# Hybrid decoder trunk on one Trainium2 core: when projections, table loads and the last gate columns are issued

## Chip, cores and metric

The kernel runs on one core of a Trainium2 chip. The metric is device time in microseconds (us), the median of several executions; less is better. On the engines: PE is TensorE, DVE is VectorE, ACT is ScalarE, POOL is GpSimd, SP is SyncE.

## What is computed

Two identical layers over 512 tokens of width 1024, in float32. `rms_norm` divides by the root mean square; `swiglu` is the feed-forward part. Cut to what matters:

```python
for l in range(DEPTH):                      # DEPTH = 2
    u = rms_norm(x, ln1[l]) @ w_in[l]       # all mixers' inputs and four gates, one product
    y_a = forgetting_attention(...)         # "fox": per-head norms of q and k, 128-query blocks
    y_b = rms_norm(gla_chunked(...)) * silu(gr)
    y_c = rms_norm(retention_chunked(...)) * silu(rg)
    y_d = rms_norm(ssd_chunked(silu(conv(xbc)), ...) * silu(z))
    g = sigmoid(gates)                      # four branches x 1024 columns
    merged = sum(g[b] * (y_b @ w_up_b))     # over the branches a, b, c, d
    x = x + merged @ w_out[l]
    x = x + swiglu(rms_norm(x, ln2[l]), w_ffn_in[l], w_ffn_out[l])
```

## The kernel before

Activations lie transposed in SBUF: 128 partitions of features by 512 tokens, eight such blocks for a row of width 1024. Float32 products are built from float32r pieces: `split` casts a tile to a high part on ACT (L217) and takes the rest as a low part on DVE (L218), and a product of two split operands is three matmuls (`mm`, L203: high by high, low by high, high by low). A projection (`proj`) of 128 columns is eight blocks of three, so 24 matmuls of 128x512 into one PSUM bank named `mm` (four of these banks); the mixers use four other banks named `mx`.

Weights come in slabs of 128x1024 by SP's DMA into `wr` (two buffers). A slab is split into `wh` and `wl` (three buffers each), so ACT's cast of a slab waits until PE has done with the slab three earlier. The feed-forward part and part of `w_in` go through Strassen products, whose low parts are formed by an ACT scaling (L522) and an accumulating DMA from POOL (L523).

ACT holds one set of function tables at a time. `act` puts a table load (L236) ahead of a function from another set and ties the order of the functions with tables: Ln and Exp share a set, Silu and Sin share one, Sigmoid has its own.

One layer runs in this order: the norm of x and its column sums; four projections of C_X side by side (`group`) and two more, each evacuated by DVE with a multiply (L716); a Strassen part; then the four mixers ssd, gla, ret and fox. A mixer is a Python generator: `drain` runs it, and at each yield `pull` takes entries from the list `fill`, each with a cost in us, until the budget PACE of that mixer is used. The entries are independent work for PE: projections of the gate columns (`gate_quad`, four projections each, evacuated at L1370, then a Sigmoid on ACT over a pair tile `k`, 128x1024), projections with a Silu (`silus`), and up-projections (`ups`, evacuated at L1386). What is left over is issued behind fox by `pull(1e9)`.

This sets only the order in which the program is written. The framework's scheduler (`schedule_with_timeline_sim=True`, in `kernel`) then puts the instructions of each engine into a fixed sequence by its own model of time; on the chip each engine works its sequence off in order. SBUF tiles come from pools with fixed counts; `TT()` takes a 128x512 tile from the pool `tp`.

In fox, `fox_squares` squares the four q and k tiles and splits them (L217, L218); a pair of matmuls for each sums the squares over a head (`mx<-t,cr`), Ln and Exp on ACT and three steps on DVE (`newton`, L372 to L374) make the inverse root, and L1247 applies it. `stack` prepares a head (L1255 to L1265), `score` makes a block of scores (DVE L1277 and L1280, Exp on ACT, DVE L1283 and L1284), `value` transposes it (L1293), splits it and multiplies it with v (`mx<-t,t`), and `finish` adds two halves (ACT L1308, DVE L1309) and splits the result `ya`, from which the up-projections of branch a start.

Of the kernel before, what the change touches and what calls it, by code (L numbers as in the profile page):

```python
# [13 lines left out]
AF = mybir.ActivationFunctionType  # L14
# [4 lines left out]
P = 128  # L19
S = 512  # L20
D = 1024
KD = D // P
# [11 lines left out]
C_Z, C_X, C_DT, C_G = 2836, 3348, 4116, 4124  # L34
# [3 lines left out]
WARM = 11  # L38
TILE = 5.2
LAG = 1  # L40
PACE = (4.5, 5.0, 5.0, 7.5)
WIDE = 256 + 28
PARTS = (6, 6, 6, 4)
PLAIN = 2
# [88 lines left out]
def trunk(ctx: ExitStack, tc: tile.TileContext, keys, qkeys, xin, pos, wst, wsq, par, ext, cst, out):  # L133
    nc = tc.nc
# [14 lines left out]
    def nm(s):  # L149
        uid[0] += 1  # L150
        return f"{s}{uid[0]}"

    def pad(pool, n):
        pool.tile([P, n // 4], F32, tag=nm("pad"), name=nm("pad"))
# [8 lines left out]
    def phase(**bufs):  # L163
        st = ExitStack()
        for n, b in bufs.items():
            pools[n] = st.enter_context(tc.tile_pool(name=nm(n), bufs=1 if n[0] == "g" else b, reuse_waits="tile"))
            if n[0] == "g":
                pad(pools[n], b)
            st.callback(pools.pop, n)
        return st  # L170
# [10 lines left out]
    def KT(shape, dtype=F32):  # L181
        return pools["kp"].tile(shape, dtype, tag="k", name=nm("k"))
# [7 lines left out]
    def MM():  # L190
        return pm.tile([P, S], F32, tag="mm", name=nm("mm"))

    def MX():
        return px.tile([P, S], F32, tag="mx", name=nm("mx"))
# [10 lines left out]
    def mm3(o, l, r, start, stop):  # L205
        (lh, ll), (rh, rl) = l, r
        mm(o, lh, rh, start, False)
        mm(o, lh, rl, False, False)
        mm(o, ll, rh, False, stop)
# [19 lines left out]
    def order(a, b):  # L229
        tc.add_manual_dep(a.ins, b.ins.name, mybir.DependencyInfo(mybir.DependencyClass.NoSync, mybir.DependencyReason.DATA), reason="table")  # L230

    def act(out, in_, func, **kw):
        want = {AF.Ln: "natural_log_exp_and_others", AF.Exp: "natural_log_exp_and_others", AF.Silu: "silu_and_others", AF.Sin: "silu_and_others", AF.Sigmoid: "sigmoid_and_others"}.get(func)
        pre = None
        if want and want != seen["set"]:
            pre = A.preload_act_table_set(want)  # L236
            if seen["last"] is not None:
                order(pre, seen["last"])
            seen["set"] = want
            seen["pre"] = pre  # L240
        i = A.activation(out=out, in_=in_, func=func, **kw)  # L241
        if want:
            order(i, seen["pre"])
            seen["last"] = i
        return i
# [184 lines left out]
    def group(name, l, cols, src, nk, hook=None):  # L430
        ps = [MX() for _ in cols]
        for k in range(nk):
            if hook and k in hook:
                hook[k]()
            for i, c in enumerate(cols):
                mm3(ps[i], block(name, l, k, c), src[k], k == 0, k == nk - 1)
        return ps

    def proj(name, l, c, src, nk):
        ps = MM()  # L440
        for k in range(nk):
            mm3(ps, block(name, l, k, c), src[k], k == 0, k == nk - 1)
        return ps
# [173 lines left out]
    def layer(l, n1, scopes):  # L617
        outer, scope = scopes
# [6 lines left out]
        fill = []  # L625
# [10 lines left out]
        def drain(gen, us):  # L636
            for want in gen:
                pull(us * (1 if want is None else want))

        def mix(a, b):  # L640
            n = max(len(a), len(b))
            return [t for i in range(n) for l_ in (a, b) for t in l_[i:i + 1]]
# [32 lines left out]
        gates = {}  # L675
# [32 lines left out]
            begin(-2)  # L708

        ps4 = group("w_in", l, [C_X + P * i for i in range(4)], n1, KD, {4: first, 5: lambda: next(steps), 6: third, 7: fourth})  # L710
        n1.rstd(True)
        for i in range(0, 6, 2):
            t = KT([P, 2, S])
            for j in range(2):
                ps = ps4[i + j] if i < 4 else proj("w_in", l, C_X + P * (i + j), n1, KD)
                V.tensor_tensor(out=t[:, j], in0=ps, in1=n1.r, op=ALU.mult)  # L716
                cin[i + j] = t[:, j]
        cap[0] = len(keys) // SLAB + FRONT // SLAB - 6
        run()
        scope.close()  # L720
        scope = phase(vp=2, bd=1, tp=24)
        vp = pools["vp"]
        sbd = pools["bd"].tile([P, 7, 2, P], F32, name=nm("sbd"))
        G.memset(sbd, 0.0)
# [82 lines left out]
        ps = MX()  # L807
# [538 lines left out]
        def silus(name, c, tiles):  # L1346
            def go(i):
                def f():
                    if i == 0:
                        gates[name] = tiles()  # L1350
                    t = gates[name][i]
                    V.tensor_tensor(out=t, in0=proj("w_in", l, c + P * i, n1, KD), in1=n1.r, op=ALU.mult)
                    act(out=t, in_=t, func=AF.Silu)
                return f
            return [(TILE, go(i)) for i in range(2)]

# [4 lines left out]
        def gate_quad(b, q):  # L1361
            st = {}

            def go(i):
                def f():
                    if i % 2 == 0:
                        st["t"] = KT([P, 2, S])
                        gates.setdefault(b, []).append(st["t"])
                    ps = proj("w_in", l, C_G + b * D + (4 * q + i) * P, n1, KD)
                    V.tensor_tensor(out=st["t"][:, i % 2], in0=ps, in1=n1.r, op=ALU.mult)  # L1370
                    if i % 2:
                        act(out=st["t"], in_=st["t"], func=AF.Sigmoid)
                return f
            return [(TILE, go(i)) for i in range(4)]

# [19 lines left out]
        def up_of(b, q):  # L1395
            ys_, name = {0: (ya, "w_up_a"), 1: (yb, "w_up_b"), 2: (yc, "w_up_c"), 3: (yd, "w_up_d")}[b]
            return ups(b, ys_, name, q, b == 3, b == 0)
# [3 lines left out]
        if l == 0:  # L1401
            rotary()
        drain(ssd(), PACE[0])
        fill += gate_quad(3, 1) + mix(silus("rg", C_RG, lambda: [TT(), TT()]), up_of(3, 0))
        fill += [keep(fq, j, C_FQ + P * j) for j in range(2)] + [keep(fk, j, C_FK + P * j) for j in range(2)]
        drain(gla(), PACE[1])
        fill += [(0.0, fox_sums)] + tokmajor(fv, C_FV, True) + [(0.0, fox_rows)]
        fill += mix(gate_quad(1, 0), up_of(3, 1)) + mix(gate_quad(1, 1), up_of(1, 0))
        drain(ret(), PACE[2])
        fill += mix(gate_quad(2, 0), up_of(1, 1)) + mix(gate_quad(2, 1), up_of(2, 0)) + mix(gate_quad(0, 0), up_of(2, 1)) + gate_quad(0, 1)  # L1410
        drain(fox(), PACE[3])
        fill += up_of(0, 0) + up_of(0, 1)
        pull(1e9)

        n2 = Norm(PR("ln2"), 16)
# [16 lines left out]
        scope = phase(g=128, tq=1, ep=8, rp=5, g0=64, lp=2, g1=384, fp=9)  # L1432
# [25 lines left out]
        ps4 = group("w_ffn_in", l, [0, FFN, P, FFN + P], n2, KD, {4: hook})  # L1458
# [10 lines left out]
        for part, n in enumerate(PARTS):  # L1469
# [17 lines left out]
            ps4 = [MX() for _ in range(4)]  # L1487
# [8 lines left out]
            for d in range(4, KD):  # L1496
                ps = MM()
# [10 lines left out]
    n1 = Norm(pr[:, 0, o:o + w])  # L1508
# [4 lines left out]
    for l in range(DEPTH):  # L1513
        n1 = layer(l, n1, scopes if l == 0 else front())
# [71 lines left out]
```

## Time and profile before

| what | value |
|---|---|
| median of 3 runs | 1767.44 us (1767.35 to 1768.34) |
| the profiled execution | 1772.7 us, span of its records 1770.8 us |
| mean granted clock of TensorE | 0.985 |
| PE busy | 1726.9 us, 98% |
| DVE, ACT, POOL busy | 1250.3, 972.5, 244.5 us |
| table loads (L236) | 80, of 1283 ns each |

The profiled execution is 5.3 us above the median, and 1.9 us of it lie outside the span. A row of the timeline gives start and duration, engine, line, operation, output and inputs, and in brackets the idle time before it and what ended that. Matmuls overlap: a duration of 0.39 us with starts 0.23 us apart means one matmul every 0.23 us. The windows' table gives, for each stretch, its length, the busy time of PE, PE's weight loads, DVE, ACT and POOL with their counts in parentheses, and then the granted TensorE clock (1.00 is full speed), the share of the DMA engines and GB/s.

### The profile page before, as it was taken

How to read it: one execution, taken by the hardware profiler on the slowest of the kernel's cores; microseconds unless marked ns; L12 is line 12 of the kernel's file. 1: busy time of each engine (PE TensorE's matmuls, PEld its weight loads, DVE VectorE, ACT ScalarE, POOL GpSimd, SP SyncE). 2: the span in 40 equal slices, each digit the busy share in tenths (PEclk: the TensorE clock that was granted, in tenths of full speed). 3: DMA queues.
4: the chain of work that ended last, by engine and by line, in shares of the span. 5: the costliest groups of instructions: out<-in, count | busy, mean ns of one | idle time of the engine just before them, and what ended most of it. 6: DMA issues, size and time to landing. Idle time of an engine off the chain costs nothing.

```text
span 1770.8 us, 25962 instructions
## 1 busy us (share of the span) xinstructions
PE 1726.9 (98%) x10428; PEld 1503.6 (85%) x10428; DVE 1250.3 (71%) x1739; ACT 972.5 (55%) x1329; POOL 244.5 (14%) x239
## 2 busy tenths in 40 slices
PE   8999999989989999999999999998998999999998
PEld 6988888768878989898979878886787789999998
DVE  6795776687658767675787766656776687676766
ACT  7656552466637646464665456325656376464643
POOL 2103112022101000000011042010221010101010
PEclk9999999999989999999999999999999899999999
DMA  7432222212215757575344322222122147575743
GB/s 247 96 117 75 72 72 84 81 63 84 84 61 154 191 131 183 133 184 120 96 143 108 107 61 84 82 76 82 60 87 81 60 145 201 128 185 131 188 109 106
DMA packets 56424, 201.34 MB, mean 114 GB/s; under 512 B 6256, under 2 KB 6640, under 8 KB 56304
## 3 DMA queue, kind: packets, MB, share of 16 engines
q1 hardware_dynamic: 45072, 160.45, 28.4%
q0 software_dynamic: 10368, 37.75, 12.1%
q8 instruction: 82, 1.34, 0.3%
q10 hardware_dynamic: 864, 1.48, 0.2%
q14 instruction: 38, 0.31, 0.1%
HBM read 197.56 MB, written 2.10 MB: 113 GB/s over the span
## 4 chain that ended last, share of the span: by engine, by line
PE 85%; DVE 6%; ACT 5%; issue 3%; DMA 1%; POOL 0%; ACTq 0%; POOLq 0%
PE mm L203 55%; PE mx L203 29%; DVE wl L218 1%; ACT L236 1%; ACT wh L217 1%; ACT t L241 1%; ACT k L241 1%; ACT t L217 0%; DVE xl L399 0%; DMA wl<-in_wsq_dram 0%; DVE x L1481 0%; PE mx L1293 0%; DVE f L1480 0%; DVE rq L513 0%; ACT xh L241 0%
## 5 line engine op out<-in xcount | busy, mean ns | idle before, releaser
L217 ACT CAST wh<-wr 128x1024 fp32r<-128x1024 f32 (+1 forms) x228 | 237.2, 1041 | 309.4 <-PE mm L203 159.6
L203 PE MATMUL mm<-xh,wh 128*128 128x512 f32 (+1 forms) x1088 | 389.7, 358 | 1.7 <-DVE k L1370 1.4
L203 PE MATMUL mm<-xh,wl 128*128 128x512 f32 (+1 forms) x1088 | 389.2, 358 | 1.1 <-DVE wl L218 1.1
L203 PE MATMUL mm<-xl,wh 128*128 128x512 f32 (+1 forms) x1088 | 388.3, 357 | 0.0
L218 DVE TENSOR_TENSOR wl<-wr,wh 128x1024 fp32r<-128x1024 f32 (+1 forms) x204 | 254.6, 1249 | 100.5 <-ACT wh L217 98.9
L203 PEld LDWEIGHTS mm<-xh,wh 128*128 128x128 f32 x1088 | 206.4, 190 | 32.2 <-DVE k L1370 1.3
L203 PEld LDWEIGHTS mm<-xh,wl 128*128 128x128 f32 x1088 | 205.8, 189 | 32.4 <-DVE wl L218 2.0
L203 PEld LDWEIGHTS mm<-xl,wh 128*128 128x128 f32 x1088 | 206.3, 190 | 29.3 <-issue 0.5
L203 PE MATMUL mx<-xh,wh 128*128 128x256 f32 (+1 forms) x512 | 154.3, 310 | 6.0 <-ACT wh L217 5.0
L203 PE MATMUL mx<-xl,wh 128*128 128x256 f32 (+1 forms) x512 | 157.5, 308 | 0.0
L203 PE MATMUL mm<-t,wh 128*128 128x512 f32 x448 | 146.8, 405 | 9.2 <-ACT t L217 4.1
L523 POOL DMA_DIRECT2D wl<-in_wsq_dram x70 | 60.4, 864 | 597.9 <-ACT wl L522 403.7
L218 DVE TENSOR_TENSOR l<-rq,wh 128x1024 fp32r<-128x1024 f32 x72 | 87.9, 1221 | 40.7 <-ACT wh L217 24.8
L203 PEld LDWEIGHTS mm<-t,wh 128*128 128x128 f32 x448 | 85.1, 193 | 29.2 <-ACT t L217 4.5
L203 PE MATMUL mx<-f,wh 128*128 128x512 f32 x352 | 108.2, 390 | 0.0
L203 PEld LDWEIGHTS mx<-xh,wh 128*128 128x128 f32 x512 | 97.2, 190 | 12.6 <-ACT wh L217 6.1
L203 PE MATMUL mm<-f,wh 128*128 128x512 f32 x352 | 105.9, 389 | 0.0
L217 ACT CAST wh<-rq 128x1024 fp32r<-128x1024 f32 x72 | 75.5, 1048 | 51.2 <-PE mm L203 22.4
L236 ACT ACT_TABLE_LOAD x80 | 102.6, 1283 | 1.3
L203 PEld LDWEIGHTS mx<-xl,wh 128*128 128x128 f32 x512 | 97.3, 190 | 5.4
L203 PE MATMUL mx<-xh,wl 128*128 128x256 f32 (+1 forms) x304 | 95.4, 325 | 0.8 <-DVE wl L218 0.4
L203 PE MATMUL mm<-t,wl 128*128 128x512 f32 x224 | 89.7, 400 | 0.0
(308 smaller groups left out, 3816.2 us busy)
## 6 DMA issues: line engine op xcount, KB each, us to landing
wr<-in_wst_dram SPq DMA_DIRECT2D x200, 512.0 KB, 3.5
rq<-in_wsq_dram SPq DMA_DIRECT2D x72, 512.0 KB, 5.6
wl<-in_wsq_dram POOLq DMA_DIRECT2D x70, 512.0 KB, 6.5
wr<-in_wsq_dram SPq DMA_DIRECT2D x24, 512.0 KB, 7.0
out_dram<-x SPq DMA_DIRECT2D x8, 256.0 KB, 2.0
x<-in_x_dram SPq DMA_DIRECT2D x3, 512.0 KB, 6.4
wr<-in_wst_dram SPq DMA_DIRECT2D x4, 256.0 KB, 5.4
l<-in_wsq_dram POOLq DMA_DIRECT2D x2, 512.0 KB, 6.9
```

Of the source, the lines that this page charges most:

```text
L203: T.matmul(o, lhsT=l, rhs=r, start=start, stop=stop, skip_group_check=True)
L217: A.copy(out=hi, in_=src)
L218: V.tensor_tensor(out=lo, in0=src, in1=hi.bitcast(F32), op=ALU.subtract)
L236: pre = A.preload_act_table_set(want)
L241: i = A.activation(out=out, in_=in_, func=func, **kw)
L523: G.dma_start(out=lo, in_=wsq[j], accum_op=ALU.add)
```

## The change

Seven edits. PACE goes from 4.5, 5, 5, 7.5 to 4.4, 4.9, 4.9, 7.2. The fifth projection of C_X is written ahead of `n1.rstd(True)`, so its matmuls may stand between the group and the norm's column sums. The mixers' pool `tp` gets 28 tiles instead of 24 (8 KB more of each partition). Both Silus of a `silus` pair are issued with the second projection, and both Sigmoids of a `gate_quad` with its fourth. The last two projections of the last `gate_quad(0, 1)` are taken out of the list that fox pulls from and written behind fox, ahead of branch a's up-projections. The memory set aside for the descriptors of dynamic transfers is 8192 instead of 16384 bytes, so tiles lie 8 KB lower.

```diff
-PACE = (4.5, 5.0, 5.0, 7.5)
+PACE = (4.4, 4.9, 4.9, 7.2)
...
         ps4 = group("w_in", l, [C_X + P * i for i in range(4)], n1, KD, {4: first, 5: lambda: next(steps), 6: third, 7: fourth})
+        ps4.append(proj("w_in", l, C_X + 4 * P, n1, KD))
         n1.rstd(True)
...
-                ps = ps4[i + j] if i < 4 else proj("w_in", l, C_X + P * (i + j), n1, KD)
+                ps = ps4[i + j] if i + j < 5 else proj("w_in", l, C_X + P * (i + j), n1, KD)
...
-        scope = phase(vp=2, bd=1, tp=24)
+        scope = phase(vp=2, bd=1, tp=28)
...
                     V.tensor_tensor(out=t, in0=proj("w_in", l, c + P * i, n1, KD), in1=n1.r, op=ALU.mult)
-                    act(out=t, in_=t, func=AF.Silu)
+                    if i:
+                        for t in gates[name]:
+                            act(out=t, in_=t, func=AF.Silu)
...
-                    if i % 2:
-                        act(out=st["t"], in_=st["t"], func=AF.Sigmoid)
+                    if i == 3:
+                        for t in gates[b][-2:]:
+                            act(out=t, in_=t, func=AF.Sigmoid)
...
-        fill += mix(gate_quad(2, 0), up_of(1, 1)) + mix(gate_quad(2, 1), up_of(2, 0)) + mix(gate_quad(0, 0), up_of(2, 1)) + gate_quad(0, 1)
+        last_quad = gate_quad(0, 1)
+        fill += mix(gate_quad(2, 0), up_of(1, 1)) + mix(gate_quad(2, 1), up_of(2, 0)) + mix(gate_quad(0, 0), up_of(2, 1)) + last_quad[:2]
         drain(fox(), PACE[3])
-        fill += up_of(0, 0) + up_of(0, 1)
+        fill += last_quad[2:] + up_of(0, 0) + up_of(0, 1)
...
-    nc = _bacc.Bacc("TRN2", target_bir_lowering=False, num_devices=1)
+    nc = _bacc.Bacc("TRN2", target_bir_lowering=False, num_devices=1, dynamic_dma_scratch_size=8192)
```

The scheduler orders all engines anew. In ACT's sequence the rows at L236 go from 80 to 48. Lines of the changed file are up to 5 higher: L1370 becomes L1373, L1386 becomes L1390, L1247 becomes L1248, L1308 becomes L1309.

**Place 1, the start of fox in layer 0.** ACT before, from the cast of a slab to the last of the four squares (t_3173, t_3179, t_3185 and t_3191 in this listing are the squares; wh608 and wh617 are slabs, t540 and t543 belong to the norm of ret's heads):

```order
L217 CAST wh608_3408<-wr607_3406 128x1024
L217 CAST t540_3111<-t537_3099 128x512
L217 CAST wh617_3456<-wr616_3454 128x1024
L217 CAST t543_3122<-t538_3102 128x512
L241 ACTIVATE t551_3173<-t425_2486 128x512
L217 CAST t552_3175<-t551_3173 128x512
L241 ACTIVATE t554_3179<-t432_2525 128x512
L217 CAST t555_3181<-t554_3179 128x512
L241 ACTIVATE t557_3185<-t453_2601 128x512
L217 CAST t558_3187<-t557_3185 128x512
L241 ACTIVATE t560_3191<-t462_2646 128x512
```

ACT after; the slab cast of the same place is wh617, the squares are t545, t548, t551, t554:

```order
L217 CAST t543_3116<-t538_3096 128x512
L241 ACTIVATE t545_3120<-t427_2486 128x512
L217 CAST t546_3122<-t545_3120 128x512
L241 ACTIVATE t548_3126<-t448_2562 128x512
L217 CAST t549_3128<-t548_3126 128x512
L241 ACTIVATE t551_3132<-t457_2607 128x512
L217 CAST t552_3134<-t551_3132 128x512
L241 ACTIVATE t554_3138<-t466_2656 128x512
L217 CAST wh617_3448<-wr616_3446 128x1024
L217 CAST t555_3140<-t554_3138 128x512
```

The cast of slab wh617 stood ahead of all squares and of the last split of ret's norm; it now stands behind three squares, ahead of the fourth's cast. In PE's sequence the last matmuls of that norm (`mx<-t,cr`) were followed by 4 matmuls of one gate projection, 6 of an up-projection and 24 of the next projection; now by 5, 24, 6 and 24. Behind them come 6 of an up-projection and the fox norms as before, but these 6 now stand between the second norm's two matmuls, and the stack's matmul stands ahead of the next gate projection (g2qa below) instead of inside it.

DVE before, from the last split of a square on; mm563 is the bank of an up-projection which g2qa takes over:

```order
L218 TENSOR_TENSOR t562_3194<-t560_3191,t561_3193 128x512
L1386 TENSOR_TENSOR t567_3210<-mm563_3197,k493_2831 128x512
L372 SCALAR_TENSOR_TENSOR t581_3271<-mx573_3249,t577_3261 128x512
L372 SCALAR_TENSOR_TENSOR t582_3277<-mx574_3252,t578_3264 128x512
L373 SCALAR_TENSOR_TENSOR t581_3271<-t581_3271,t577_3261 128x512
L373 SCALAR_TENSOR_TENSOR t582_3277<-t582_3277,t578_3264 128x512
```

DVE after; the same bank is mm576 here, read in the row at L1390 with t580:

```order
L218 TENSOR_TENSOR t556_3141<-t554_3138,t555_3140 128x512
L372 SCALAR_TENSOR_TENSOR t572_3214<-mx564_3193,t568_3205 128x512
L372 SCALAR_TENSOR_TENSOR t573_3220<-mx565_3196,t569_3207 128x512
L373 SCALAR_TENSOR_TENSOR t572_3214<-t572_3214,t568_3205 128x512
L373 SCALAR_TENSOR_TENSOR t573_3220<-t573_3220,t569_3207 128x512
L372 SCALAR_TENSOR_TENSOR t574_3226<-mx566_3199,t570_3209 128x512
L374 SCALAR_TENSOR_TENSOR t568_3205<-t572_3214,t568_3205 128x512
L372 SCALAR_TENSOR_TENSOR t575_3232<-mx567_3202,t571_3211 128x512
L1390 TENSOR_TENSOR t580_3250<-mm576_3237,k497_2839 128x512
L1390 TENSOR_TENSOR t586_3292<-mm585_3285,k497_2839 128x512
L1390 TENSOR_TENSOR t593_3335<-mm592_3328,k521_2998 128x512
```

The evacuation that frees the bank stood ahead of the Newton steps of the fox norms; it now stands behind seven of them, the first step of the fourth norm (t575) among them, and two more evacuations follow it at once.

**Place 2, the end of fox in layer 0.** ACT before, from the Exp of the last block of scores (t823) on; k817 is a gate pair tile, t831 and t834 are the split of the transposed scores, t836 to t837 the finish:

```order
L241 ACTIVATE t823_4446,frs825_4453<-t823_4446,fmx824_4451 128x512
L236 ACT_TABLE_LOAD
L241 ACTIVATE k817_4410<-k817_4410 128x1024
L236 ACT_TABLE_LOAD
L217 CAST t831_4496<-mx830_4491 128x512
L217 CAST t834_4508<-mx833_4504 128x384
L1308 COPY t836_4516<-mx813_4397 64x512
L217 CAST t837_4519<-t719_3951 128x512
```

ACT after; the last Exp is t814, the gate pairs are k808 and k830, the split is t822 and t825, the finish t827 and t828:

```order
L241 ACTIVATE t814_4364,frs816_4371<-t814_4364,fmx815_4369 128x512
L236 ACT_TABLE_LOAD
L241 ACTIVATE k808_4328<-k808_4328 128x1024
L217 CAST wh860_4572<-wr859_4570 128x1024
L241 ACTIVATE k830_4439<-k830_4439 128x1024
L236 ACT_TABLE_LOAD
L217 CAST t822_4412<-mx821_4407 128x512
L217 CAST t825_4424<-mx824_4420 128x384
L1309 COPY t827_4432<-mx802_4305 64x512
L217 CAST t828_4435<-t713_3894 128x512
```

Between the last Exp and the split stood a table load, a Sigmoid and a table load; now a slab cast (wh860) and a second Sigmoid stand there too. PE, between the last score and the products of the split (`mx<-t,t`, eight matmuls), had 8 matmuls of the last gate projection and 12 of the up-projections of branch a; now it has all 24 of the last projection and 12 of the up-projections. In layer 1 the last score stood behind the whole projection and 9 matmuls of the up-projections, with 3 left between it and the products; after, both layers have the order of layer 0. The wait of wh860 is for the last projection's last matmul, and that of Sigmoid k830 for that projection's evacuation on DVE.

**Place 3, the norm of layer 1.** PE before, from the last matmuls of the group on; mm1511 is the bank of the norm's sum, mm1522 that of the fifth projection:

```order
L203 MATMUL mx1484_8507<-xl1428_8279,wh1495_8581 128x512
L203 MATMUL mx1484_8507<-xh1427_8278,wl1496_8582 128x512
L203 MATMUL mm1511_8674<-n1512_8675,cr_123 128x512
L203 MATMUL mm1514_8681<-cs_122,n1437_8343 128x1 x4
L203 MATMUL mm1522_8708<-xh1427_8278,wh1507_8638 128x512
L203 MATMUL mm1522_8708<-xl1428_8279,wh1507_8638 128x512
L203 MATMUL mm1522_8708<-xh1427_8278,wl1508_8639 128x512
L203 MATMUL mm1522_8708<-xh1427_8278,wh1507_8638 128x512
```

PE after; the fifth projection is mm1511, the sum mm1515:

```order
L203 MATMUL mx1484_8491<-xl1428_8263,wh1495_8565 128x512
L203 MATMUL mx1484_8491<-xh1427_8262,wl1496_8566 128x512
L203 MATMUL mm1511_8658<-xh1427_8262,wh1507_8622 128x512
L203 MATMUL mm1511_8658<-xl1428_8263,wh1507_8622 128x512
L203 MATMUL mm1515_8689<-n1516_8690,cr_123 128x512
L203 MATMUL mm1518_8696<-cs_122,n1437_8327 128x1 x4
L203 MATMUL mm1511_8658<-xh1427_8262,wl1508_8623 128x512
L203 MATMUL mm1511_8658<-xh1427_8262,wh1507_8622 128x512
```

Two of the fifth projection's matmuls now precede the sum; the third, which reads the slab's low part, follows it.

## Prediction

> **What bounds it now.** I read the page first: the share of each engine, the chain that ended last, the table loads.
>
> ```profile
> span 1770.8 us, 25962 instructions
> PE 1726.9 (98%) x10428; PEld 1503.6 (85%) x10428; DVE 1250.3 (71%) x1739; ACT 972.5 (55%) x1329; POOL 244.5 (14%) x239
> PE 85%; DVE 6%; ACT 5%; issue 3%; DMA 1%; POOL 0%; ACTq 0%; POOLq 0%
> L236 ACT ACT_TABLE_LOAD x80 | 102.6, 1283 | 1.3
> ```
>
> PE is busy for 98%, and the chain lies on it for 85%. The change takes no matmul away, so it can win only what PE waits (1770.8 - 1726.9 = 43.9 us) and what PE loses at a lower clock. Next I asked the windows where that is: the start of fox and its end, in layer 0 and in layer 1.
>
> ```profile
> 345.00:400.00 55.00, 48.06 (x194) 36.81 (x193) 45.16 (x66) 35.06 (x48) 11.73 (x9) 0.94 0.21 67
> 478.00:510.00 32.00, 27.46 (x114) 22.10 (x113) 18.71 (x30) 13.17 (x19) 0.58 (x2) 0.84 0.21 65
> 1220.00:1275.00 55.00, 48.81 (x194) 37.05 (x193) 43.31 (x65) 35.29 (x49) 9.21 (x8) 0.94 0.20 62
> 1355.00:1390.00 35.00, 28.15 (x116) 22.20 (x115) 18.35 (x31) 16.88 (x24) 1.45 (x2) 0.80 0.19 60
> ```
>
> In these 177 us PE idles for 6.94 + 4.54 + 6.19 + 6.85 = 24.5 us, over half of all. The clock column gives the rest: (1 - 0.94) x 55 = 3.3, (1 - 0.84) x 32 = 5.1, again 3.3, and (1 - 0.80) x 35 = 7.0 us of full clock not granted. The timeline of PE at the start of fox, layer 0, shows each wait and both speeds:
>
> ```profile
> 351.40 0.39 PE L203 MATMUL mm<-xl,wh 128*128 128x512 f32 x1
> 351.63 0.39 PE L203 MATMUL mm<-xh,wl 128*128 128x512 f32 x1
> 353.49 0.73 PE L203 MATMUL mm<-t,wh 128*128 128x512 f32 x2 [1.47 <-DVE k L1370]
> ...
> 358.21 0.50 PE L203 MATMUL mx<-t,cr 128*128 128x512 f32 x1 [3.07 <-ACT t L217]
> ...
> 364.11 0.63 PE L203 MATMUL mm<-xh,wl 128*128 128x512 f32 x1
> 364.54 0.63 PE L203 MATMUL mm<-xh,wh 128*128 128x512 f32 x1
> ```
>
> A matmul follows another after 0.23 us at full clock (351.40, 351.63) and after 0.43 at the lower one (364.11, 364.54). The 1.47 us wait was not followed by the lower clock, the 3.07 us one was.
>
> **Part 1: the end of fox (the term that decides).** Timelines of PE, ACT and DVE in layer 0, and of PE in layer 1:
>
> ```profile
> 489.36 0.77 PE L1293 MATMUL mx<-cs,t 128*128 128x128 f32 x5
> 492.48 2.48 PE L203 MATMUL mx<-t,t 128*128 128x256 f32 x8 [2.35 <-ACT t L217]
> 497.00 2.50 PE L203 MATMUL mm<-t,wh 128*128 128x512 f32 x5 [2.04 <-ACT t L217]
> ```
> ```profile
> 486.40 1.05 ACT L217 CAST wh<-wr 128x1024 fp32r<-128x1024 f32 x1 [4.33 <-issue]
> 487.35 0.72 ACT L241 ACTIVATE t<-t,fmx 128x512 f32<-128x512 f32 x1
> ...
> 488.18 1.28 ACT L236 ACT_TABLE_LOAD   x1
> 489.48 1.06 ACT L241 ACTIVATE k<-k 128x1024 f32<-128x1024 f32 x1
> 490.55 1.28 ACT L236 ACT_TABLE_LOAD   x1
> 491.85 0.97 ACT L217 CAST t<-mx 128x512 fp32r<-128x512 f32 x2
> 495.00 0.58 ACT L1308 COPY t<-mx 64x512 f32<-64x512 f32 x1 [2.19 <-PE mx L203]
> 496.33 0.62 ACT L217 CAST t<-t 128x512 fp32r<-128x512 f32 x1 [0.75 <-DVE t L1309]
> ```
> ```profile
> 484.39 0.75 DVE L1277 SCALAR_TENSOR_TENSOR t<-mx,cq,t 128x512 f32<-128x512 f32 x1 [1.41 <-PE mx L203]
> ```
> ```profile
> 1369.58 1.33 PE L1293 MATMUL mx<-cs,t 128*128 128x128 f32 x5 [2.25 <-DVE t L1284]
> 1373.12 2.48 PE L203 MATMUL mx<-t,t 128*128 128x256 f32 x8 [2.22 <-ACT t L217]
> 1377.70 2.50 PE L203 MATMUL mm<-t,wh 128*128 128x512 f32 x5 [2.09 <-ACT t L217]
> ```
>
> The split at 491.85 has its input from 490.13 (489.36 + 0.77), yet stands behind a Sigmoid between two table loads. What it costs now: layer 0 waits 2.35 + 2.04, and of the 10.2 us at half clock (twice 5.1) some 2.0 are idle, so 8.2 us do 4.1 us' worth; 2.35 + 2.04 + 4.1 = 8.5. Layer 1 waits 2.25 + 2.22 + 2.09, and 14.0 us at half clock less 4.3 idle cost 4.8: 11.4.
>
> After, by the new order with these durations, counted from the score's end S (484.2, before DVE's 484.39): the Exp starts at S + 3.15 and ends at S + 3.9 (487.35 + 0.72); a slab cast and the table load run by then as before. The cast wh860 must wait for the last of 24 projection matmuls, S + 6.3 (24 x 0.23 and three small ones, and 0.4 to drain). The first Sigmoid is done by S + 6.3 too (3.9 + 0.2 + 1.28 + 1.06). Then the cast 1.05, Sigmoid 1.06, load 1.28: S + 9.7; the products follow 0.65 later (491.83 to 492.48), S + 10.3. PE is ready for them after 36 matmuls of 0.23 and about 1.0 of small ones, S + 9.3. So one wait of about 1.0 us stays of the first, in both layers. The finish (product, copy L1308, L1309, cast) is not touched: 2.04 stays, nothing is put behind it. Whether 1.0 and 2.0 with 0.9 us of products between them lower the clock, no row shows; it costs from nothing to the present 4.1 and 4.8, and I take 2.0, in the middle. New cost per layer 1.0 + 2.04 + 2.0 = 5.0. Gain 8.5 - 5.0 + 11.4 - 5.0 = **9.9 us**, ends 5.0 (clock as now) and 13.9 (full clock). The two projections put behind fox thus help by standing inside this wait: 36 instead of 20 matmuls of cover, for 2.1 us more of ACT work.
>
> Here 2.35 and 2.04 in succession did lower the clock (0.84 in the window), while 1.47 alone did not. The Trainium skill ("TensorE: Matmul & The Clock Gate", HAM oscillation) asks for no idle gap over about 3.4 us; by it neither wait would lower the clock, and the gain would be the 13.9 end. On waits of this length this trace does not agree with it.
>
> **Part 2: the start of fox.** ACT and DVE in layer 0:
>
> ```profile
> 354.95 1.04 ACT L217 CAST wh<-wr 128x1024 fp32r<-128x1024 f32 x1 [4.06 <-PE mm L203]
> 356.36 0.62 ACT L217 CAST t<-t 128x512 fp32r<-128x512 f32 x1 [0.36 <-DVE t L851]
> ...
> 361.62 1.84 ACT L241 ACTIVATE t<-mx,cs 128x512 f32<-128x512 f32 x3
> 363.33 1.15 ACT L241 ACTIVATE t<-t 128x512 f32<-128x512 f32 x2
> ```
> ```profile
> 356.19 1.22 DVE L218 TENSOR_TENSOR wl<-wr,wh 128x1024 fp32r<-128x1024 f32 x1
> ...
> 362.35 0.68 DVE L1386 TENSOR_TENSOR t<-mm,k 128x512 f32<-128x512 f32 x1
> 364.00 1.29 DVE L372 SCALAR_TENSOR_TENSOR t<-mx,t 128x512 f32<-128x512 f32 x2 [0.97 <-ACT t L241]
> ```
>
> Now the squares are late because the slab cast (354.95) waited 4.06 us for PE and everything on ACT queued behind it: PE waits 1.47 + 3.07 and loses 3.3 by the clock; of the window's other 2.4 us of idle time I let 1.0 go, since two more evacuations now follow the first at once on DVE: 8.8 per layer. After, three squares stand ahead of that cast, and PE has 24 more matmuls (5.5 us) before the fox norms: both waits go. What is late next: the fourth square's split, behind cast wh617 (1.04 + 0.62 on ACT, a slab's low part 1.22 and the split 0.7 on DVE, from about 0.2 after the up-projection's last matmul), against 0.9 us of PE work: about 2.4 us. Then the next gate projection needs a bank that DVE frees only behind the fourth norm's first Newton step: Ln 0.61, two Exp 1.15, L372 0.65, L1390 0.68 and 0.3 of hand-overs, less one matmul, 3.2 us. 5.6 us of waits and some 3.3 of clock: 8.9. **Nothing is won, 0 us**; ends -4 and +6 for both layers.
>
> **Part 3: the fifth projection.** PE at the norm of layer 1:
>
> ```profile
> 910.22 0.50 PE L203 MATMUL mm<-n,cr 128*128 128x512 f32 x1 [2.73 <-ACT n L217]
> ...
> 912.73 0.80 PE L203 MATMUL mm<-xh,wl 128*128 128x512 f32 x1 [0.58 <-DVE wl L218]
> ```
>
> Two of its matmuls now run in the 2.73 us, but the third still waits for the slab's low part until 912.73. The two waits end where they did: 0, at most -0.5 (two matmuls).
>
> **Part 4: the rest.** 32 of 80 table loads go, 41 us of ACT at 1.283; ACT has 45% idle, so most of it is hidden, and parts 1 and 2 have what I could place. PE's other waits are 43.9 - 24.5 = 19.4 us, the program's start and part 3 included. Fewer loads may win some, but a pair of Sigmoids now holds ACT for 4.7 us (2 x 1.28 + 2 x 1.06) instead of 3.6: **-2 us**, ends -6 and +5. "ScalarE: Activation LUTs" of the Trainium skill (What ACT_TABLE_LOAD costs) adds a drain of 1.38 us to each load's 1.28, which would double ACT's saving; here the Sigmoid starts 0.02 us behind its load (488.18 + 1.28, 489.48), so no drain is added. The smaller PACE and the four tiles: 0, since the list is empty before the fox ends either way, and no wait of the rows above is for a `tp` tile.
>
> ```profile
> L523 POOL DMA_DIRECT2D wl<-in_wsq_dram x70 | 60.4, 864 | 597.9 <-ACT wl L522 403.7
> wl<-in_wsq_dram POOLq DMA_DIRECT2D x70, 512.0 KB, 6.5
> ```
>
> Half the descriptor memory touches only these 70 accumulating transfers. POOL idles 597.9 us before them, mostly for ACT, so a later issue has room; were one held until the last landed (6.5 us), a few would reach PE. 0, up to +3; a gain has no row to come from.
>
> **Sum.** -9.9 + 0 + 0 - 2 = -12 us, 1772.7 to 1760.7 of the profiled execution, which is 5.3 above the median: 1767.44 to **1755**.
>
> **Rivals.** *All waits at both places go, with the clock:* 8.5 + 11.4 + 2 x 8.8 = 37.5, 1730. For it: half of ACT's excursions are gone. Against: the finish's 2.04 us is untouched. *The clock stays up at fox's end:* 1.0 and 2.0 are too short for it; the gain there is 13.9 and the whole -16, 1751. For it: 1.47 us did nothing. Against: 2.35 and 2.04 sufficed. This is what the skill's rule above gives.
>
> *It does not do what it says:* the scheduler puts the last projections almost where they were, and every wait moves on by one; 0, 1767. For it: parts 2 and 3. Against: 36 matmuls against 20, and in layer 1 against 3. *Slower, by the bank at fox's start:* if the evacuation waits for all seven Newton steps ahead of it and not only for the last, 6 x 0.65 = 3.9 us are added per layer, and a half-clock stretch 1.7 more, 11 for both; with the 5 of part 1's low end that gives +6, 1773. It decides as soon as ACT's Ln rows start more than 3 us later than PE is done with the third norm. For it: DVE works in order, and nothing else is ready behind. Against: the first three norms' sums come before the slab cast.
>
> **Chances.** My case 0.51, the clock stays up 0.15, all waits gone 0.05, no change 0.12, slower 0.17. What a measurement of this kernel can tell from no change is 0.2%, 3.5 us. With every term at its better end the sum is -13.9 - 4 - 0.5 - 6 = -24.4, 1743; that is the low end, and leaves out the first rival. At their worse ends the terms give -5 + 6 + 5 + 3 = +9, beyond the slower rival's +6; I cut at +3.6, 1771, which holds no change and leaves out most of the slower cases, some 0.12. My case alone I put at -4 to -20. Faster 0.71, same 0.12, slower 0.17.
>
> **What would show it.** Part 1: 36 matmuls after the last score, then a wait near 1 us, one near 2.0, and a clock above 0.84 and 0.80 in these windows. Part 2: no wait at the first fox norm, 2 to 3 us at the fourth, 3 us before the next gate projection behind DVE's L1390. Part 3: the third matmul waits for `wl`. I am wrong if the two end windows gain under 5 us, or if the start windows lose more than 6.

## The result, and the profile after

The changed kernel takes 1756.49 us (median of 4 runs, 1755.23 to 1758.37), the kernel before 1767.8 beside it (4 runs, 1767.35 to 1768.34): ratio 0.9928, interval 0.9916 to 0.9941. The ratio is the recorded one; the two medians by themselves give 0.9936, inside the interval. 1755 was predicted. From its page the span, the share of each engine and the chain that ended last:

```profile
span 1753.8 us, 25909 instructions
PE 1715.4 (98%) x10428; PEld 1498.2 (85%) x10428; DVE 1263.3 (72%) x1739; ACT 929.4 (53%) x1295; POOL 251.8 (14%) x239
PE 91%; DVE 4%; ACT 3%; DMA 1%; issue 1%; POOL 0%; ACTq 0%
```

The table loads at L236, from the groups by line:

```profile
L236 ACT ACT_TABLE_LOAD x48 | 61.6, 1283 | 0.8
```

ACT makes 48 instead of 80. The chain now lies on PE for 91% instead of 85%. The windows of the same four stretches (start and end of fox, layer 0 and layer 1):

```profile
338.00:393.00 55.00, 48.47 (x204) 38.39 (x203) 48.60 (x73) 30.42 (x47) 10.36 (x9) 0.94 0.25 77
471.00:503.00 32.00, 29.09 (x129) 23.48 (x128) 21.05 (x33) 14.79 (x21) 4.24 (x3) 0.95 0.22 66
1209.00:1264.00 55.00, 48.48 (x206) 38.43 (x205) 48.42 (x71) 30.12 (x47) 10.74 (x9) 0.94 0.26 77
1342.00:1374.00 32.00, 29.09 (x130) 23.46 (x129) 21.09 (x33) 14.39 (x20) 4.25 (x3) 0.95 0.20 66
```

At the end of fox PE idles 2.91 us in both layers (4.54 and 6.85 before), at a clock of 0.95 (0.84 and 0.80). At the start it idles 6.5 us, about as before, at the same clock. What is left at the end, in PE's timeline of layer 0:

```profile
487.53 0.38 PE L203 MATMUL mx<-t,t 128*128 128x256 f32 x1 [0.53 <-ACT t L217]
488.25 1.03 PE L203 MATMUL mx<-t,t 128*128 128x256 f32 x7 [0.34 <-DVE t L218]
491.32 1.43 PE L203 MATMUL mm<-t,wh 128*128 128x512 f32 x5 [2.04 <-ACT t L217]
```

and ACT's at the same place:

```profile
482.61 1.06 ACT L241 ACTIVATE k<-k 128x1024 f32<-128x1024 f32 x1
483.58 1.04 ACT L217 CAST wh<-wr 128x1024 fp32r<-128x1024 f32 x1
484.52 1.05 ACT L241 ACTIVATE k<-k 128x1024 f32<-128x1024 f32 x1
485.59 1.28 ACT L236 ACT_TABLE_LOAD   x1
486.89 0.97 ACT L217 CAST t<-mx 128x512 fp32r<-128x512 f32 x2
```

The wait of 2.35 us is down to 0.53 and 0.34, though ACT's path to the split got longer by a cast and a Sigmoid: PE had more to do meanwhile. The finish's 2.04 us stands. At the start of fox, layer 0:

```profile
355.88 0.49 PE L203 MATMUL mx<-t,cr 128*128 128x512 f32 x1 [0.72 <-ACT t L217]
357.22 0.49 PE L203 MATMUL mx<-t,cr 128*128 128x512 f32 x1 [0.85 <-DVE t L218]
358.96 0.47 PE L203 MATMUL mx<-t,cr 128*128 128x512 f32 x1 [1.24 <-DVE t L372]
363.07 0.79 PE L203 MATMUL mm<-xh,wh 128*128 128x512 f32 x1 [3.64 <-DVE t L1390]
```

DVE's rows ahead of the last of these waits:

```profile
358.12 1.29 DVE L372 SCALAR_TENSOR_TENSOR t<-mx,t 128x512 f32<-128x512 f32 x2 [0.95 <-ACT t L241]
359.33 1.28 DVE L373 SCALAR_TENSOR_TENSOR t<-t,t 128x512 f32<-128x512 f32 x2
360.53 0.68 DVE L372 SCALAR_TENSOR_TENSOR t<-mx,t 128x512 f32<-128x512 f32 x1
361.13 0.68 DVE L374 SCALAR_TENSOR_TENSOR t<-t,t 128x512 f32<-128x512 f32 x1
361.73 0.68 DVE L372 SCALAR_TENSOR_TENSOR t<-mx,t 128x512 f32<-128x512 f32 x1
362.33 1.88 DVE L1390 TENSOR_TENSOR t<-mm,k 128x512 f32<-128x512 f32 x3
```

The waits ahead of the first norm (1.47 and 3.07) are gone. In their place PE waits 0.72 and 0.85 us for the two halves of the fourth square's split. The third wait, 1.24, is of the stack's matmul, for a bank that the first Newton step frees. The fourth, 3.64, is for the bank of the up-projection: its evacuation at L1390 starts when DVE has done seven Newton steps without a gap, from 358.12 on. The norm of layer 1:

```profile
903.91 0.50 PE L203 MATMUL mm<-xh,wh 128*128 128x512 f32 x1 [2.21 <-ACT wh L217]
...
906.93 0.80 PE L203 MATMUL mm<-xh,wl 128*128 128x512 f32 x1 [1.22 <-DVE wl L218]
```

2.21 + 1.22 us, where 2.73 + 0.58 stood: the wait is the same, divided otherwise.

### The profile page after: what moved, and what is told of

It reads as the page before. It is cut to its first block, busy times and chain, and to the rows that moved or that the text cites. A ratio compares the mean times of both kernels' runs of the same rounds, so it can differ in the third digit from the quotient of the medians.

```text
span 1753.8 us, 25909 instructions
## 1 busy us (share of the span) xinstructions
PE 1715.4 (98%) x10428; PEld 1498.2 (85%) x10428; DVE 1263.3 (72%) x1739; ACT 929.4 (53%) x1295; POOL 251.8 (14%) x239
## 4 chain that ended last, share of the span: by engine, by line
PE 91%; DVE 4%; ACT 3%; DMA 1%; issue 1%; POOL 0%; ACTq 0%
PE mm L203 60%; PE mx L203 30%; ACT wh L217 1%; ACT k L241 1%; DVE wl L218 0%; PE mx L1294 0%; DVE xl L399 0%; DVE rq L513 0%; ACT L236 0%; DVE t L218 0%; DMA wl<-in_wsq_dram 0%; DVE x L1486 0%; DVE f L1485 0%; ACT xh L241 0%; ACT n L241 0%
## 5 line engine op out<-in xcount | busy, mean ns | idle before, releaser
L218 DVE TENSOR_TENSOR wl<-wr,wh 128x1024 fp32r<-128x1024 f32 (+1 forms) x204 | 258.5, 1268 | 116.5 <-ACT wh L217 115.3
L203 PE MATMUL mm<-t,wh 128*128 128x512 f32 x448 | 142.8, 397 | 4.2 <-ACT t L217 4.1
L203 PEld LDWEIGHTS mm<-f,wh 128*128 128x128 f32 x352 | 66.1, 188 | 13.6
```

The source lines that it names most:

```text
L203: T.matmul(o, lhsT=l, rhs=r, start=start, stop=stop, skip_group_check=True)
L218: V.tensor_tensor(out=lo, in0=src, in1=hi.bitcast(F32), op=ALU.subtract)
```

## The experiments

Two theories were tested. Cover: the gain is PE work that now lies between the last score and its products, and the rest is order. Table loads: the gain is the 32 loads that ACT no longer makes. Two facts needed no run, since the scheduler's sequences tell them. The kernel before with only the `last_quad` edit has the sequences of before on PE, ACT and DVE, row for row. The changed kernel without it differs in 18 rows of PE at the end of fox, and in none of ACT and DVE. There one transposing matmul (L1294) comes eight places later in each layer, and the others move up by one. Alone, that edit therefore gains nothing; in the changed kernel it can hardly matter.

All results, with PE's idle time in the two stretches at the start of fox (55 us each) and the two at its end (32 us each), from the windows of each profile:

| kernel | median us | ratio to before (interval) | idle, starts | idle, ends |
|---|---|---|---|---|
| before, again | 1768.16 | one run | 7.08 + 6.59 | 4.74 + 7.50 |
| changed | 1756.49 | 0.9928 (0.9916 to 0.9941) | 6.53 + 6.52 | 2.91 + 2.91 |
| tables_only | 1756.72 | 0.9927 (0.9913 to 0.9941) | 4.84 + 4.55 | 4.74 + 4.50 |
| no_tables | 1758.11 | 0.9934 (0.9918 to 0.9949) | 6.23 + 6.53 | 3.45 + 3.60 |
| pace_only | 1770.94 | 1.0004 (0.9995 to 1.0013) | 11.08 + 11.18 | 4.01 + 4.02 |
| pace_undone | 1755.98 | 0.9919 (0.9906 to 0.9931) | 4.22 + 4.21 | 4.54 + 4.41 |
| memory_only | 1761.38 | 0.9952 (0.9940 to 0.9965) | 3.64 + 3.83 | 7.21 + 7.21 |
| memory_undone | 1772.04 | 1.0014 (1.0004 to 1.0023) | 11.09 + 11.32 | 2.92 + 2.92 |
| descriptors_only | 1769.86 | 0.9996 (0.9987 to 1.0005) | 6.59 + 6.51 | 4.73 + 7.50 |
| fifth_undone | 1757.08 | 0.9926 (0.9913 to 0.9938) | 6.22 + 6.24 | 2.91 + 2.91 |
| fox_pace_6_6 | 1750.34 | 0.9890 (0.9874 to 0.9905) | 7.43 + 7.16 | 0 + 0 |
| early_bank | 1752.87 | 0.9904 (0.9890 to 0.9919) | 2.75 + 4.29 | 4.16 + 4.02 |
| early_bank_6_6 | 1743.45 | 0.9852 (0.9839 to 0.9865) | 3.51 + 3.45 | 0 + 0 |

Ratios go against runs of the kernel before on the same chip; there its median was 1769.8 to 1770.3, beside the changed kernel 1767.8. Medians of different rows can therefore differ by some 2 us for the chip alone, and rows are better compared by their ratios.

The fifth projection and the `last_quad` edit turn out to be worth nothing, so the rows from before to memory_undone hold all eight combinations of three edits: paired Silus and Sigmoids, PACE, tiles (with the smaller descriptor memory, worth nothing by itself). Pairs alone 0.9927, PACE alone 1.0004, tiles alone 0.9952; pairs and PACE 1.0014 (memory_undone), pairs and tiles 0.9919 (pace_undone), PACE and tiles 0.9934 (no_tables), all three 0.9928. No combination gains more than the pairs alone by more than its interval, and PACE without the tiles takes the pairs' gain away.

**The kernel before, again.** No edit.

> The kernel before, profiled once more. The profiled execution on which the prediction was worked out is 1772.7 us, 5.3 above its median of 1767.4. If the half-clock stretches are a matter of where the waits fall (theory: luck of the clock), this profile shows the same waits at the four places (2.35 and 2.04 us at the end of fox in layer 0, 2.25, 2.22 and 2.09 in layer 1) but shorter half-clock stretches, and a time near 1767. Rival: the profiled execution is always some 5 us longer than the median; then it is again near 1772 with the same stretches.

1768.16 us, span 1766.2 against 1770.8 of the first profile. The windows of the end of fox:

```profile
475.00:507.00 32.00, 27.26 (x117) 21.92 (x116) 18.29 (x30) 14.58 (x20) 0.59 (x2) 0.89 0.21 66
1354.00:1386.00 32.00, 24.50 (x101) 19.13 (x100) 17.16 (x28) 14.76 (x21) 1.45 (x2) 0.84 0.17 50
```

The clock is 0.89 and 0.84 instead of 0.84 and 0.80. The waits stand at the same places, but PE idles 4.74 and 7.50 us there instead of 4.54 and 6.85. PE in layer 0 and in layer 1 of the repeat:

```profile
490.94 0.38 PE L203 MATMUL mx<-t,t 128*128 128x256 f32 x1 [2.35 <-ACT t L217]
491.67 1.04 PE L203 MATMUL mx<-t,t 128*128 128x256 f32 x7 [0.34 <-DVE t L218]
```
```profile
1365.44 0.77 PE L1293 MATMUL mx<-cs,t 128*128 128x128 f32 x5 [2.24 <-DVE t L1284]
1368.99 2.48 PE L203 MATMUL mx<-t,t 128*128 128x256 f32 x8 [2.78 <-ACT t L217]
```

In the first profile the lower clock had begun one step earlier in both layers. In layer 0 the eight products took 2.48 us there, and here they are over in 1.77 (491.67 + 1.04 - 490.94), of which 0.34 are a wait. In layer 1 the five transposing matmuls took 1.33 us there and 0.77 here, and the wait behind them is longer here by the same 0.56 (2.78 for 2.22): while PE has to wait for the chain anyway, the lower clock costs nothing. So the same program gets half-clock stretches of different length from one execution to the next, and the first profile was a long one: its PE is busy for 7.3 us more than in the repeat and idle for 2.7 less. Spans of this profile and of the one after differ by 12.4 us, near the 11.3 of the medians, and not by 17.0.

**Table loads alone, and all but them.**

```diff
# tables_only: before, with
-                    act(out=t, in_=t, func=AF.Silu)
+                    if i:
+                        for t in gates[name]:
+                            act(out=t, in_=t, func=AF.Silu)
...
-                    if i % 2:
-                        act(out=st["t"], in_=st["t"], func=AF.Sigmoid)
+                    if i == 3:
+                        for t in gates[b][-2:]:
+                            act(out=t, in_=t, func=AF.Sigmoid)
# no_tables: the changed kernel with these lines the other way round
```

> The kernel before with only the two edits of silus and gate_quad (both Silus with the second projection, both Sigmoids with the fourth). Cover theory (the gain comes from PE work between the last score and the products): only 13 matmuls of the last projection and 12 of the up-projections stand there in both layers, 25 against 36 after the whole change, so the first wait at the end of fox is about 3 to 3.6 us instead of 0.87, no better than before; the gain against before is small, 1764 to 1768. Table theory (fewer table loads are the gain): 56 loads instead of 88 as in the whole change, so most of the 11 us are there: 1755 to 1760.

> The changed kernel with the edits of silus and gate_quad undone (78 table loads in all instead of 54). Cover theory: 21 matmuls of the last projection and 12 of the up-projections stand ahead of the products, 33 against 36, with the same sequence on ACT, so the first wait is about 1.5 us and the end of fox keeps its gain: 1757 to 1761. Table theory: back to the time before, 1764 to 1768.

Each theory missed once. tables_only has the whole gain, 1756.72, where the cover theory gave 1764 to 1768; no_tables keeps it too, 1758.11, where the table theory gave 1764 to 1768. The profile of tables_only shows that it gets there by another road:

```profile
340.00:395.00 55.00, 50.16 (x204) 38.51 (x202) 44.74 (x67) 31.63 (x47) 10.04 (x9) 0.94 0.22 68
473.00:505.00 32.00, 27.26 (x116) 21.36 (x115) 17.12 (x27) 13.55 (x19) 0.58 (x2) 0.89 0.22 66
```

The end of layer 0 idles 4.74 us, no better than before, as the cover theory had it; that of layer 1 went from 7.50 to 4.50. The start won 2 us per layer: ahead of fox ACT has no Sigmoid between two loads any more. The end of no_tables, with 33 matmuls of cover, idles 3.45 and 3.60, also as the cover theory had it. In the four stretches tables_only idles 7.3 us less than the repeat of before, and the clock there is worth at most 1.6 more; of the 11.4 us between the spans, another 1.4 are a wait inside fox of layer 1, at this place of the repeat:

```profile
1331.84 0.85 PE L203 MATMUL mx<-t,t 128*128 128x256 f32 x3 [1.42 <-ACT t L217]
```

ACT came to that split late because a load, a Sigmoid and a second load stood ahead of it from 1323.28 on, and ACT has no gap from there to the split; in tables_only and in the changed kernel the wait is gone. So each theory tells the waits that it is about, and neither tells the time: the gains overlap, and without the one edit the others still shorten much the same waits.

**PACE and memory.** Each alone on the kernel before, and each undone in the changed kernel.

```diff
# pace_only: before, with          (pace_undone: the changed kernel, the other way round)
-PACE = (4.5, 5.0, 5.0, 7.5)
+PACE = (4.4, 4.9, 4.9, 7.2)
# memory_only: before, with        (memory_undone: the changed kernel, the other way round)
-        scope = phase(vp=2, bd=1, tp=24)
+        scope = phase(vp=2, bd=1, tp=28)
...
-    nc = _bacc.Bacc("TRN2", target_bir_lowering=False, num_devices=1)
+    nc = _bacc.Bacc("TRN2", target_bir_lowering=False, num_devices=1, dynamic_dma_scratch_size=8192)
# descriptors_only: before, with the last line alone
```

> The kernel before with the new PACE alone. With ret's smaller budget the up-projection whose bank the first gate projection needs is written behind fox's norms, and the row that evacuates it stands behind the Newton steps on DVE, as in memory_undone. Bank theory: the start of fox loses some 17.5 us per layer as there (12.5 before), the end loses less (27 matmuls of cover in both layers, about 7.8 us each against 8.9 and 11.8), in sum 3 to 7 us slower than before: 1771 to 1776. Rival (PACE does nothing by itself): 1766 to 1770.

> The changed kernel with the old PACE (4.5, 5, 5, 7.5). The sequence has 13 instead of 24 matmuls of the last projection ahead of the products at the end of fox, in both layers. Cover theory: the first wait there is 0.87 + 11 x 0.23 = 3.4 us instead of 0.87, the window's loss as in tables_only (7.8 and 7.7 us), so 3 to 6 us more than the changed kernel: 1759 to 1763. Theory that any new order is about as good as another: within 2 us of the changed kernel, 1755 to 1759.

> The kernel before with 28 tiles in the mixers' pool and 8 KB for descriptors. PE's sequence has 24 more matmuls between ret's norm and fox's norms, as after the whole change, and the bank's evacuation stands ahead of the Newton steps; at the end only 3 matmuls of cover in both layers, as in layer 1 of before. Cover theory: the start loses some 7 to 9 us per layer instead of 12.5, the end of layer 0 about 3 more: 4 to 9 us faster than before, 1760 to 1765. Rival (the tiles help only where the new PACE hurts): 1767 to 1770.

> The changed kernel with 24 tiles in the mixers' pool and 16 KB for descriptors. The end of fox has the same sequences on PE and ACT; the mixers' order differs. If descriptors and tiles cost and bring nothing, 1755 to 1759. If the four tiles carry the gain: 1764 to 1768. If the smaller descriptor memory held transfers up in the changed kernel, this one is 1 to 3 us faster and the median time of POOL's transfers to landing is below 6.3 us.

> The kernel before with 8 KB instead of 16 KB for descriptors and nothing else; the sequences of PE, ACT and DVE are those of before, row for row. If descriptors cost nothing: the time of before, 1766 to 1771, ratio within 0.2% of 1. If POOL's transfers are held up by the smaller memory: 1 to 3 us slower and their median time to landing above 6.5 us.

This was the surprise: memory_undone has nothing of the gain (1772.04, ratio 1.0014), and is above every range that was given for it. Its start of fox, windows and PE's waits:

```profile
350.00:405.00 55.00, 43.91 (x172) 33.40 (x171) 43.75 (x67) 28.75 (x44) 8.82 (x8) 0.84 0.19 62
```
```profile
360.37 0.49 PE L203 MATMUL mx<-t,cr 128*128 128x512 f32 x1 [2.61 <-ACT t L217]
...
367.00 0.77 PE L203 MATMUL mx<-t,cr 128*128 128x512 f32 x1 [1.56 <-DVE t L372]
373.64 0.80 PE L203 MATMUL mm<-xh,wh 128*128 128x512 f32 x1 [5.87 <-DVE t L1390]
```

11.09 us of idle time per start and a clock of 0.84. The 5.87 us are the wait for the bank, of the slower rival, in full. pace_only has it as well:

```profile
369.61 0.79 PE L203 MATMUL mm<-xh,wh 128*128 128x512 f32 x1 [5.87 <-DVE t L1386]
```

With ret's smaller budget the up-projection that holds the bank is written behind fox's norms instead of ahead of them, and its evacuation falls behind the Newton steps. By itself this costs the start what it wins at the end (11.1 idle instead of about 6.8; 4.0 instead of 4.74 and 7.50): 1770.94, no change, where 1771 to 1776 was expected. pace_undone is as fast as the changed kernel, with 13 matmuls of cover (4.54 idle at the end) and no wait for the bank (4.22 at the start). The cover theory's 1759 to 1763 was missed there: it counted what the end loses and not what the start wins. PACE moves the loss from one place to the other.

memory_only is faster, 1761.38:

```profile
343.00:398.00 55.00, 51.36 (x206) 39.52 (x206) 43.28 (x66) 36.40 (x51) 9.83 (x9) 0.94 0.22 67
476.00:508.00 32.00, 24.79 (x103) 19.95 (x102) 17.85 (x28) 14.80 (x21) 1.45 (x2) 0.84 0.16 49
```

Its start idles 3.64 us instead of 7.08, its end 7.21 in layer 0 too, which had 4.74: both as the cover theory said, from the 24 more matmuls ahead of fox's norms and the 3 at its end. With four tiles more the scheduler can put ret's last steps and its norm earlier. The descriptor memory is no part of it. With 24 tiles the sequences are the same for 8 and 16 KB, and descriptors_only, whose order is that of before, takes 1769.86, with this time to landing:

```profile
wl<-in_wsq_dram POOLq DMA_DIRECT2D x70, 512.0 KB, 6.6
```

6.5 in the first profile, 6.3 in the changed one. Halving it is free; what it buys is the room, as 28 tiles beside 16 KB do not fit.

**The fifth projection.**

```diff
# fifth_undone: the changed kernel, with
-        ps4.append(proj("w_in", l, C_X + 4 * P, n1, KD))
...
-                ps = ps4[i + j] if i + j < 5 else proj("w_in", l, C_X + P * (i + j), n1, KD)
+                ps = ps4[i + j] if i < 4 else proj("w_in", l, C_X + P * (i + j), n1, KD)
```

> The changed kernel with the fifth projection of C_X back behind the norm's sum. Part 3 of the prediction says nothing is won by it: 1755 to 1758. Rival (two matmuls in the wait and the freed order are worth something): 1758 to 1761.

1757.08: nothing, as part 3 said.

**The two waits that were left.**

```diff
# fox_pace_6_6: the changed kernel, with
-PACE = (4.4, 4.9, 4.9, 7.2)
+PACE = (4.4, 4.9, 4.9, 6.6)
# early_bank: the changed kernel, with
             yield 0.7
             fox_squares()
-            yield
+            yield 2
...
-            yield 2
+            yield 1
# early_bank_6_6: both
```

> The changed kernel with PACE for fox at 6.6 instead of 7.2. More of the fill is left behind fox: 57 matmuls of projections stand between the last score and the products or among them, and 11 between the products and the first matmul that needs the finish. The start of fox is the same in PE's sequence up to the first gate projection. Cover theory: the waits of 0.87 and 2.04 us at the end of fox go in both layers, and with them the half clock (1.6 us each by the window's 0.95): about 9 us less than the changed kernel, 1746 to 1750. Rival (fox itself is starved): with less fill between its scores PE waits for softmax steps in the middle of fox, and the time is the changed kernel's or more, 1756 to 1762.

> The changed kernel with one edit: fox yields 2 and 1 instead of 1 and 2 around its norms, so that the up-projection whose evacuation frees the bank is written ahead of the norms. On DVE the row at L1390 then stands ahead of the Newton steps; the other rows of ACT at the start of fox stay. At the end only 15 matmuls of the last projection remain ahead of the products, instead of 24. Bank theory (the 3.9 us wait of the first gate projection after the norms is for that evacuation alone): this wait goes in both layers, with some 3 us of half clock each, and the end loses some 2 us more per layer: 1745 to 1751. Rival (PE would wait there anyway, for the stack or the first scores): the 3.9 us move to the next matmul, 1756 to 1762.

> The same edit and PACE 6.6 for fox (the kernel fox_pace_6_6 ran at 1750.3 us, with 3.88 us still waited behind L1390 in each layer). Bank theory: 2 x 3.9 us and up to 2 x 3 us of half clock less, 1738 to 1743. Rival (moved on): 1748 to 1752.

fox_pace_6_6 takes 1750.34, a gain of 6 where 9 was expected. The end of fox in layer 0:

```profile
469.00:501.00 32.00, 32.00 (x152) 26.64 (x151) 20.15 (x30) 16.56 (x21) 2.67 (x3) 1.00 0.27 91
```

No idle time and full clock, so the cover theory is right in full here. The rest was paid inside fox, where less fill is left, at one place above all:

```profile
444.05 0.72 PE L203 MATMUL mm<-t,wh 128*128 128x512 f32 x2 [1.46 <-DVE k L1373]
```

early_bank takes 1752.87. The 3.64 us are gone and the start idles 2.75 and 4.29. A part moved on, as the rival had it, to the first scores, 0.85 us in layer 0 and in layer 1 this:

```profile
1245.97 0.80 PE L203 MATMUL mx<-t,t 128*128 128x128 f32 x2 [2.40 <-ACT t L1260]
```

The end has 15 matmuls of cover instead of 24 and idles 4.16 and 4.02: 1752.87 is 2 us above the range that was expected. Together the two are worth more than their sum, 1743.45, just above the 1738 to 1743 that was expected (by the medians 13.0 us less than the changed kernel, against 6.2 and 3.6), since the lower PACE keeps the end covered:

```profile
332.00:387.00 55.00, 51.49 (x217) 40.80 (x216) 47.47 (x72) 32.08 (x49) 8.51 (x8) 0.97 0.25 77
465.00:497.00 32.00, 32.00 (x152) 26.64 (x151) 20.28 (x29) 16.48 (x20) 2.44 (x2) 1.00 0.27 86
```

This kernel beats both, by 1.5% and by 0.75%: ratio to before 0.9852 (0.9839 to 0.9865).

## Why the prediction was right, and where not

The time, 1756.5 for 1755, and the place, the end of fox, were right. By its steps:

- **Part 1, the waits: right.** A first wait of 1.0 us was worked out and 0.53 + 0.34 = 0.87 came; 2.04 stayed 2.04, in both layers. The order of after together with the durations of before gave this to 0.15 us. That it is the cover which ends such a wait is shown by fox_pace_6_6, where more of it leaves no wait and full clock at the end.
- **Part 1, the clock: between the ends, as taken.** In this profile 0.05 of 32 us, 1.6 us of clock, are lost, for 2.0. It varies: fifth_undone has the same idle time there (2.91) and 0.89 in both layers, 3.5 us.
- **Part 1, the cause: wrong.** "The two projections put behind fox thus help by standing inside this wait" fails. Moving them in the list changes no row of before, and all but none of after. The cover came from the other edits: each of the paired Sigmoids, PACE and the tiles changes the order in which the scheduler works off the fill. Of the last gate projection 8 and 0 matmuls stood there before; 13 stand there in both layers with the pairs alone, 15 with PACE alone, none with the tiles alone, 21 with PACE and tiles, 24 with the pairs and PACE, with tiles or without. I read the cause off the edit's wording, though the order of the kernel with that edit alone would have shown it.
- **Part 2: right in sum, not wait by wait.** 2.4 us were worked out for the fourth square's split and 1.57 came (0.72 + 0.85). 3.2 us were worked out from there to the next gate projection, and 1.24 + 3.64 came. The step that fails is that DVE would be kept by the last norm's step alone: it had seven to do, one behind the other, which is what the slower rival said. The sign that I had named for that, ACT's Ln rows over 3 us late, did not appear: they start 0.6 us behind PE's third norm (355.74, 355.16). Two errors of opposite sign gave 6.45 for 5.6. The idle time of the start (6.5 us for 6.9 and 6.2) and its clock (0.94) are those of before, so nothing was won.
- **Part 3: right.** The third matmul waits for `wl`, and fifth_undone shows no price.
- **Part 4: "the smaller PACE and the four tiles: 0" failed.** No wait in the trace is for a `tp` tile, and that was no ground to price the tiles at nothing: they change where the scheduler can put work. Tiles alone are worth 0.48% (0.35 to 0.60). PACE with 24 tiles brings the bank's wait in full, 5.87 us, and the tiles cut it to 3.64. By themselves and on the others' ground the two terms are far from zero. They met in the order of the whole change, which parts 1 and 2 had read off, and that is why the sum held: it priced the order and not the edits. The descriptors' 0 was right.
- **The slower rival** was real: its wait stands in memory_undone and pace_only, at the place named, and takes back the gain of the other edits there (2.3 and 0.7 us above the kernel before beside them, for the 6 that it was priced at). In the changed kernel its mechanism is there too, and the four tiles keep the wait at 3.64 us.
- **The size of the sum: in part luck.** -12 us was set against one profiled execution that had some 5 us more than the median, and part 1 took its clock, 0.84 and 0.80, as what before costs. By the same working with the repeat's waits and clock (4.73 and 7.12 us, 0.89 and 0.84) the ends would have cost some 7 and 10 us instead of 8.5 and 11.4, and the sum been about -9 (an estimate), some 2 us short of the 11.3 that came. Against the repeat PE idles 8.2 us less over the whole span (46.6 to 38.4) and is busy for 4.2 less (1719.6 to 1715.4), together the 12.4 us. Of the idle time 7.0 lie in the four stretches (25.9 to 18.9), 6.4 of them at the ends (12.2 to 5.8). The clock lost at the ends went from 8.6 to 3.2, so part 1, 9.9 in the sum, was worth 6.4 and up to 5.4 more; not all of that, since a lower clock costs nothing while PE waits. The other 1.2 us of idle time are what the profiles show of part 4's -2; the wait of 1.42 us inside fox of layer 1 is the greatest that went.

What stays open is what fixes the start and the length of a stretch at the lower clock: for the same program it differs from one execution to the next, and no run was made that moves a wait without changing it.

## What to carry to other kernels

Where a scheduler sets the order, an edit is priced from the order it makes and not from its text, and each edit's own order is looked at before a gain is put down to it. A wait on a fixed chain (load, Sigmoid, load, split) is shortened by what the bottleneck has left to do in that moment, so count its instructions between the chain's start and its end, and keep work back for it; here 57 matmuls of 0.23 us kept back ended the first wait, and 11 behind the products the second. Edits that shorten the same wait do not add up, and one that moves a loss elsewhere can look neutral until the edit that pays for it is removed.

## What the runs showed of the hardware

The same program, with waits at the same places (2.35 and 2.04; 2.25, 2.22 and 2.09 in the first profile), was granted 0.84 and 0.79 of full clock in one execution and 0.89 and 0.84 in another, over 32 us. By 2 x 0.05 x 32 us that moves one execution of this kernel by some 3 us (an estimate). A lower clock ahead of a wait is free: five small matmuls took 1.33 instead of 0.77 us, and the wait behind them was 2.22 instead of 2.78. Halving the memory for dynamic descriptors changed nothing that could be measured in 70 accumulating transfers of 512 KB (ratio 0.9996, 0.9987 to 1.0005).
